# The first rows of a hybrid encoder layer: where g is copied, how squares are summed, and the order of the first products on TensorE

## The chip, the core and the metric

The kernel runs on one core of a Trainium2 chip. The metric is the device time of one execution in microseconds (us). Engines are named as the profile names them: PE (TensorE, matrix products), DVE (VectorE), ACT (ScalarE), POOL (GpSimd) and SP (SyncE, which issues most DMA transfers). Each takes its own instructions in order and waits on semaphores for the others.

## What is computed

One encoder layer on x of 512 rows by 1024 channels, in float32. Cut to the part that matters here:

```python
def rms_norm(x, g):
    y = x * rsqrt(mean(x * x, axis=-1, keepdims=True) + EPS)
    return y * g

n = rms_norm(x, mix_norm_g)
proj = n @ w_in                    # 512 x 1024 times 1024 x 4608
xa, zu, zv, gate_a, gate_b = split(proj)   # 512, 1024, 1024, 1024, 1024 columns
ya = s5_branch(xa, ...)            # two scans of a state-space model
yb = sgu_branch(zu, zv, ...)       # gelu, layer norm and mixing of positions
h = x + (sigmoid(gate_a) * (ya @ w_proj_a) + sigmoid(gate_b) * (yb @ w_proj_b)) @ w_out
# then memory cross-attention, a SwiGLU FFN and a last rms_norm
```

## The kernel before

**Products.** Every product is made of three matmuls: each operand is split into a high part (`hi`, a cast to fp32r by ACT) and a low part (`lo`, the rest, a subtraction by DVE), and `mm3` (L355) adds hi x hi, hi x lo and lo x hi in PSUM. `split` (L83) issues the two, one on each engine.

**Weights.** All weights come through one plan, a list of blocks of 512 KB in the order of use. A block is loaded by SP into `wraw` (three buffers), then split into `whi` and `wlo` (three buffers each). `next_w` (L330) hands out the next block, issues loads up to three blocks ahead and splits up to two ahead. The first four blocks of the plan are the first product's: rows 256 i to 256 i + 255 of `w_in`, columns of zv from 0 to 511. They are called blocks 0 to 3 below.

**Rows.** x is loaded in four row tiles of 128 rows, `xt[:, t, :]`, between the loads of the first three weight blocks (L566 to L571). Each row tile is normalised: ACT squares it and sums along the row (`sum_sq`, L483, two halves of 512, each with a read of the accumulator), DVE adds the two sums, scales and adds EPS, POOL takes the power -1/2 (`rms_factor`, L490), DVE multiplies by that factor and by g (`rms_scale`, L508). Then PE transposes its eight 128 x 128 pieces into two PSUM banks (`to_feat`, L514, tile `ptr`), and ACT and DVE split them into `xn`, the normalised rows with channels on partitions. The banks come from two rings: `bank` (five, for sums of products) and `aux` (three).

**g.** g arrives as one row (`g_row`). PE multiplies it by a column of ones (`pg`, L579), which spreads it over all partitions in two PSUM banks. ACT copies these to `g_mix` (L581 and L591) in between the steps of the first row tile. The first row tile is scaled straight from `pg` (L583), the three others from `g_mix` (L512).

**First products.** `tokm` (L399) computes zv's first 512 columns in four banks `pt`, one for each row tile: for each weight block it goes through the four row tiles, and through the last two blocks together. Gelu follows on ACT (`zv_evac`, L1019), then the products `pf` of `feat` (L362) for xa, and so on.

**Order.** A scheduler orders the instructions of each engine after the program is written, from its own model of the time; what `in_order` marks stays in the order of the program. While `pinned` is set, splits and squares are so marked: before, from the first row tile until the squares of the fourth. Transposes and first products were not marked, so the scheduler places them. In between it also places the set-up of the S5 branch (`s5_setup`, L620): small loads (`slab`, L631, the log steps; `lrows`; `brow`; `crow`), an exponential of `slab` on ACT (L672), small transposes on PE (`plam` L637, `pbc` L657 and L664) and many small operations on DVE.

Of the kernel before, what the change touches and what calls it, by code (L numbers as in the profile page):

```python
# [9 lines left out]
F32 = mybir.dt.float32  # L10
F32R = mybir.dt.float32r
AF = mybir.ActivationFunctionType
ALU = mybir.AluOpType
# [4 lines left out]
P = 128  # L18
D = 1024
T = 512  # L20
NT = T // P
KD = D // P
M = 256
NM = M // P
EPS = 1e-6
# [10 lines left out]
OFF_V = OFF_U + GW  # L36
# [16 lines left out]
def hybrid_layer_kernel(  # L53
# [17 lines left out]
    np_ = ctx.enter_context(tc.tile_pool(name="norm", bufs=2))  # L71
# [20 lines left out]
    pinned = [False]  # L92
    in_order = tc.keep_in_program_order
# [5 lines left out]
    plan, tiles = [], []  # L99
# [252 lines left out]
    def split_w(j):  # L352
        tiles.append(plan[j][2]())
# [45 lines left out]
    def tokm(w, c0, act, nk, evac, ntok=NT, last=2, kpt=2, hooks={}, cut=None, t0=0):  # L399


        toks = range(t0, t0 + ntok)
        ps = {t: bank(f"pt{t - t0}") for t in toks}
        nw = nk // kpt
        held = []
        full = slice(0, 512)
        for wi in range(nw):
            hi, lo = next_w(w, wi * kpt, kpt, c0, 512)
            held.append((wi, hi, lo))
            if wi in hooks:  # L410
                hooks[wi]()
            if wi < nw - last:
                todo, held = held, []
                for t in toks:
                    end = cut is not None and t == ntok - 1 and wi == nw - last - 1
                    tok_block(ps[t], t, todo, act, kpt, full, wi == 0, end)
                    if end:
                        cut(None, ps[t])
                tick(1.3 * ntok)
        for t in toks:  # L420
            if cut is not None and t == ntok - 1:
                for i in range(2):
                    p = aux("pcut", (P, 256))
                    tok_block(p, t, held, act, kpt, slice(256 * i, 256 * i + 256), True, True)
                    cut(i, p)
            else:
                tok_block(ps[t], t, held, act, kpt, full, nw == last, True)
                evac(t, ps[t])
            tick(1.3 * len(held))

    def tok_block(ps, t, ws, act, kpt, cs, first, final):
        tsl = slice(t * P, (t + 1) * P)
        for i, (wi, hi, lo) in enumerate(ws):
            for k in range(kpt):
                kk = wi * kpt + k
                mm3(ps, (act[0](kk, tsl), act[1](kk, tsl)) if callable(act[0]) else
                    (act[0][:, kk, tsl], act[1][:, kk, tsl]),
                    (hi[:, k, cs], lo[:, k, cs]), first and i == k == 0,
                    final and i == len(ws) - 1 and k == kpt - 1)

    side = {"gen": None, "credit": 0.0, "rate": 0.0, "now": 0, "later": []}

# [10 lines left out]
    def tick(us=5.2):  # L453

        side["now"] += us / 5.2
        run_due()
        side["credit"] = min(side["credit"] + us * side["rate"], us)
        while side["credit"] > 0.0 and side["gen"] is not None:
            try:
                used = next(side["gen"])  # L460
            except StopIteration:
                side["gen"] = None
                return
            if used is None:
                side["credit"] = 0.0
                return
            side["credit"] -= used
# [8 lines left out]
    ident = cp.tile([P, P], F32, name="ident")  # L476
# [13 lines left out]
    def rms_factor(ss, r=None):  # L490

        ms = np_.tile([P, 1], F32, tag="ms", name="ms", bufs=2)
        if r is None:
            r = np_.tile([P, 1], F32, tag="r", name="r", bufs=2)
        nc.vector.tensor_tensor(ms, ss[:, 0:1], ss[:, 1:2], ALU.add)
        nc.vector.tensor_scalar(ms, ms, 1.0 / D, EPS, ALU.mult, ALU.add)
        nc.gpsimd.tensor_tensor(r, ms, mhalf, ALU.pow)
        return r

    HALF = (slice(0, 512), slice(512, 1024))  # L500

    def row_sums(src):
        ss = np_.tile([P, 2], F32, tag="ss", name="ss", bufs=2)
        for i in range(2):
            sum_sq(ss[:, i:i + 1], src[:, HALF[i]])
        return ss

    def rms_scale(src, g, dst, ss=None):  # L508

        r = rms_factor(row_sums(src) if ss is None else ss)  # L510
        for i in range(2):
            nc.vector.scalar_tensor_tensor(dst[:, HALF[i]], src[:, HALF[i]], r, g[:, HALF[i]], ALU.mult, ALU.mult)  # L512

    def to_feat(src, hi, lo, tsl, full=None, skip=None, part=(0, 1)):  # L514

        for q in part:
            ps = aux("ptr", (P, 4, P))
            for j in range(4):
                k = 4 * q + j
                nc.tensor.transpose(ps[:, j, :], src[:, k * P:(k + 1) * P], ident)  # L520
            if q != skip:
                split(hi[:, 4 * q:4 * q + 4, tsl], lo[:, 4 * q:4 * q + 4, tsl], ps)
            if full is not None:
                nc.scalar.copy(full[:, 4 * q:4 * q + 4, tsl], ps)
# [13 lines left out]
    def slot(tag, shape, dt, name, place=NEAR):  # L538
        n = math.prod(shape[1:])
        t = sp.tile([P, KD * T + ROOM[tag]], dt, tag=tag, name=name)[:, place[tag]:place[tag] + n]  # L540
        return t.rearrange("p (a b c) -> p a b c", a=shape[1], b=shape[2]) if len(shape) == 4 else (
            t.rearrange("p (a b) -> p a b", a=shape[1]))
# [20 lines left out]
    g_mix = np_.tile([P, D], F32, tag="gain", name="g_mix", bufs=2)  # L563
    g_row = np_.tile([1, D], F32, tag="gain", name="g_row", bufs=2)
    nc.sync.dma_start(g_row, mix_norm_g)
    xt = slot("A", (P, NT, D), F32, "xt")  # L566
# [5 lines left out]
    xn_hi, xn_lo = token_slot("xn")  # L572
    xn = (xn_hi, xn_lo)

    def first_rows():

        pg = [aux("pg") for i in range(2)]
        for i in range(2):
            in_order(nc.tensor.matmul(pg[i], ones[0:1, :], g_row[:, HALF[i]], start=True, stop=True))  # L579
        r = rms_factor(row_sums(xt[:, 0, :]))  # L580
        in_order(nc.scalar.copy(g_mix[:, HALF[0]], pg[0]))  # L581
        for i in range(2):
            in_order(nc.vector.scalar_tensor_tensor(xt[:, 0, HALF[i]], xt[:, 0, HALF[i]], r, pg[i], ALU.mult, ALU.mult))  # L583
        raw = plan[0][3].pop("raw")
        hi = wp.tile([P, 2, 512], F32R, tag="hi", name="whi", bufs=3)
        lo = wp.tile([P, 2, 512], F32R, tag="lo", name="wlo", bufs=3)
        pinned[0] = True
        for q in range(2):
            split(hi[:, q, :], lo[:, q, :], raw[:, q, :])
            if q == 0:  # L590
                in_order(nc.scalar.copy(g_mix[:, HALF[1]], pg[1]))  # L591
            to_feat(xt[:, 0, :], xn_hi, xn_lo, slice(0, P), part=(q,))
        tiles.append((hi, lo))

    first_rows()
    split_w(1)
    ss = row_sums(xt[:, 1, :])
    for t in range(1, NT):
        rms_scale(xt[:, t, :], g_mix, xt[:, t, :], ss)
        if t == 1:  # L600
            ss = row_sums(xt[:, 2, :])
        to_feat(xt[:, t, :], xn_hi, xn_lo, slice(t * P, (t + 1) * P))
        if t == 1:
            ss3 = row_sums(xt[:, 3, :])
            pinned[0] = False
        if t == 2:
            ss = ss3

# [259 lines left out]
    turned = set()  # L868
# [150 lines left out]
    def zv_evac(half):  # L1019
        def f(t, ps):  # L1020
            nc.scalar.activation(zt[:, t, half * 512:(half + 1) * 512], ps, AF.Gelu_apprx_tanh,
                                 accum_out=zsum[:, t, half:half + 1])
        return f
# [2 lines left out]
    wsr, wst = wsx[:, 0], wsx[:, 1]  # L1026
    side["gen"] = s5_program()
    side["rate"] = RATE
    tokm(w_in, OFF_V, xn, KD, zv_evac(0))

    u = s5p.tile([P, G, NCH], F32, tag="u", name="u")

# [73 lines left out]
    for h in range(H):  # L1106
        ps = bank("psv")
# [73 lines left out]
    part = slot("A", (P, KD, T), F32, "part")  # L1181
# [216 lines left out]
    sums = []  # L1398
# [218 lines left out]
    ws = []  # L1617
# [241 lines left out]
```

## Time and profile before

| what | us |
|---|---|
| median of three runs | 878.69 |
| lowest and highest | 876.64, 880.33 |
| the profiled execution: device time | 877.4 |
| the profiled execution: its span | 875.6 |
| its stage of the first rows and first products, up to the first `pf` | 42.0 |

The span goes from the first to the last instruction that the profile shows; the device time has some 1.8 us around it. A row of the timeline gives start, length, engine, line, operation, output <- inputs, shape and count; equal neighbours are merged, and an "f32" shape of a matmul may be fp32r. Brackets give the idle time before an instruction and what ended it. A row of the chain gives start, length, and engine, tile and line. A row of waits gives who waited, for whom, the sum in us, how often, and the longest.

### The profile page before, as it was taken

What the parts mean: (1) busy time and instruction counts of PE and PEld (TensorE: products, weight loads), DVE (VectorE), ACT (ScalarE), POOL (GpSimd) and SP (SyncE); (2) the same over time, 40 slices, a digit from 0 to 9 for tenths busy, and PEclk for the clock granted to TensorE, in tenths of its full rate; (3) what the DMA queues carried; (4) which work ended last, traced back from release to release, by engine and by line L of the source; (5) the groups of instructions that cost most, each with busy time, mean ns of one, the idle gap of its engine ahead of it and who ended that gap; (6) DMA issues with size and microseconds to landing.
All of it is one profiled execution on the core that took longest, in us unless ns stands there. A gap on an engine that the chain in (4) does not pass through costs nothing.

```text
span 875.6 us, 14732 instructions
## 1 busy us (share of the span) xinstructions
PE 863.1 (99%) x5760; PEld 767.7 (88%) x5760; DVE 660.8 (75%) x1072; ACT 461.7 (53%) x688; POOL 88.6 (10%) x119
## 2 busy tenths in 40 slices
PE   9999999999999999999999999999999999999996
PEld 6788888888889988889899878999999999988875
DVE  5699885999846768568757746767877768899875
ACT  5643953244255643547546535545555555656664
POOL 1002201211020001100001001101111111000010
PEclk9999999999999999999999999999999999999998
DMA  8769565888663898724678545547999898366572
GB/s 253 200 187 292 112 171 149 192 230 198 161 194 110 267 314 246 252 93 161 207 239 240 157 128 158 148 144 172 218 235 235 208 234 217 97 191 207 193 238 98
DMA packets 116488, 169.56 MB, mean 194 GB/s; under 512 B 9265, under 2 KB 81473, under 8 KB 116290
## 3 DMA queue, kind: packets, MB, share of 16 engines
q1 hardware_dynamic: 96450, 140.59, 49.2%
q0 software_dynamic: 19680, 27.50, 19.8%
q8 instruction: 45, 0.74, 0.3%
q10 hardware_dynamic: 288, 0.52, 0.2%
q14 instruction: 25, 0.20, 0.1%
HBM read 159.71 MB, written 48.73 MB: 238 GB/s over the span
## 4 chain that ended last, share of the span: by engine, by line
PE 91%; DMA 4%; DVE 2%; ACT 1%; SPq 1%; issue 1%; POOLq 0%; ACTq 0%; DVEq 0%
PE pf L358 26%; PE pt L358 17%; PE px L1156 12%; PE dx L358 7%; PE pq L1156 6%; PE dq L358 3%; PE pv L1156 3%; PE dv L358 2%; PE pz L890 2%; PE qx L1156 2%; PE bx L1156 1%; DMA e<-ed 1%; PE ptr L520 1%; PE po L358 1%; DMA slab<-in_s_log_step_dram 1%; DMA wraw<-qsum 1%
## 5 line engine op out<-in xcount | busy, mean ns | idle before, releaser
L85 ACT CAST whi<-wraw 128x1024 fp32r<-128x1024 f32 (+1 forms) x145 | 148.5, 1025 | 158.5 <-PE pf L358 54.7
L86 DVE TENSOR_TENSOR wlo<-wraw,whi 128x1024 fp32r<-128x1024 f32 (+1 forms) x145 | 172.0, 1189 | 67.1 <-ACT whi L85 66.4
L358 PE MATMUL pf<-xn,whi 128*128 128x512 f32 x448 | 140.2, 392 | 0.0
L358 PEld LDWEIGHTS pf<-xn,whi 128*128 128x128 f32 x448 | 83.7, 188 | 17.3 <-issue 0.4
L358 PE MATMUL pf<-xn,wlo 128*128 128x512 f32 x224 | 87.6, 392 | 0.0
L1156 PE MATMUL px<-fn,whi 128*128 128x256 f32 x480 | 83.3, 276 | 0.0
L1156 PEld LDWEIGHTS px<-fn,whi 128*128 128x128 f32 x480 | 72.5, 188 | 0.2
L86 DVE TENSOR_TENSOR wlo<-b,whi 128x1024 fp32r<-128x1024 f32 x40 | 48.9, 1223 | 27.8 <-ACT whi L85 27.8
L85 ACT CAST whi<-b 128x1024 fp32r<-128x1024 f32 x40 | 42.2, 1054 | 50.8 <-PE px L1156 27.7
L1156 PE MATMUL px<-fn,wlo 128*128 128x256 f32 x240 | 66.4, 277 | 0.0
L1156 PE MATMUL pq<-s,whi 128*128 128x256 f32 x320 | 55.0, 276 | 0.0
L358 PE MATMUL dx<-whi,s 128*128 128x512 f32 x170 | 53.4, 391 | 0.4 <-DVE h L1784 0.4
L86 DVE TENSOR_TENSOR wlo<-t,whi 128x1024 fp32r<-128x1024 f32 x30 | 36.7, 1225 | 19.4 <-ACT whi L85 19.4
L85 ACT CAST whi<-t 128x1024 fp32r<-128x1024 f32 x30 | 31.6, 1054 | 35.3 <-PE pv L1156 12.4
L358 PEld LDWEIGHTS pf<-xn,wlo 128*128 128x128 f32 x224 | 42.1, 188 | 8.8 <-issue 0.2
L1156 PEld LDWEIGHTS pq<-s,whi 128*128 128x128 f32 x320 | 48.1, 188 | 0.0
L358 PE MATMUL pt<-whi,xn 128*128 128x512 f32 x128 | 44.5, 415 | 0.8 <-ACT xn L85 0.8
L1156 PEld LDWEIGHTS px<-fn,wlo 128*128 128x128 f32 x240 | 45.1, 188 | 0.0
L1156 PE MATMUL pq<-s,wlo 128*128 128x256 f32 x160 | 44.2, 276 | 0.0
L358 PEld LDWEIGHTS dx<-whi,s 128*128 128x128 f32 x170 | 31.8, 188 | 7.6 <-issue 0.8
L358 PE MATMUL dx<-wlo,s 128*128 128x512 f32 x85 | 32.9, 389 | 0.0
L358 PEld LDWEIGHTS pt<-whi,xn 128*128 128x128 f32 x128 | 24.6, 195 | 6.8 <-ACT xn L85 1.4
(453 smaller groups left out, 2197.5 us busy)
## 6 DMA issues: line engine op xcount, KB each, us to landing
wraw<-in_w_in_dram SPq DMA_DIRECT2D x36, 512.0 KB, 4.9
dsum<-in_w_down_dram SPq DMA_DIRECT2D x20, 512.0 KB, 5.8
wraw<-dsum SPq DMA_DIRECT2D x20, 512.0 KB, 3.6
b<-in_w_gate_dram SPq DMA_DIRECT2D x15, 512.0 KB, 5.6
b<-in_w_up_dram SPq DMA_DIRECT2D x15, 512.0 KB, 4.6
wraw<-in_w_down_dram SPq DMA_DIRECT2D x15, 512.0 KB, 4.3
dsum<-in_w_down_dram POOLq DMA_DIRECT2D x10, 512.0 KB, 7.1
dsum<-dsum POOLq DMA_DIRECT2D x10, 512.0 KB, 8.1
```

The lines of the kernel that those rows point to most:

```text
L85: hi = nc.scalar.copy(dst_hi, src)
L86: lo = nc.vector.tensor_tensor(dst_lo, src, dst_hi.bitcast(F32), ALU.subtract)
L358: m = nc.tensor.matmul(ps, a[x], b[y], start=start and i == 0, stop=stop and i == 2, skip_group_check=free)
L520: nc.tensor.transpose(ps[:, j, :], src[:, k * P:(k + 1) * P], ident)
L890: nc.tensor.matmul(ps[:, g, :], wt[:, g, :], u[:, o * GO + g, :], start=True, stop=True)
L1156: nc.tensor.matmul(ps[:, j, :], a[x], b[y], start=start and j == k == i == 0, stop=k == 3 and i == 2, skip_group_check=True)
```

## The change

Five things change, all in the first 42 us.

- The two copies of g to `g_mix` leave the first row tile. They come behind the second row tile's splits and block 2's split (new L624). The second row tile is scaled from `pg`, as the first.
- Row tiles 2, 3 and 4 are squared in one operation of 1024 elements each (`whole_sum`), with one accumulator read, and the addition of two sums on DVE falls away. The squares themselves go to `sums`, which takes a large slot of SBUF (E) that the tile `wsx` uses afterwards.
- The first products and the transposes of row tiles 2 to 4 are marked to stay in the order of the program on PE, and that order goes by row tiles: blocks 0 and 1 with tile 1; transposes of tile 2; blocks 0 and 1 with tile 2; block 2 with tiles 1 and 2; transposes of tile 3; blocks 0 to 2 with tile 3; transposes of tile 4; blocks 0 to 2 with tile 4, and then block 3 with all four (these last two left to the scheduler).
- Block 2 is split after the second row tile's split instead of ahead of it.
- For the first two row tiles the second half's transposes take a bank of `bank`, since `pg` keeps two of `aux`.

```diff
-    def tok_block(ps, t, ws, act, kpt, cs, first, final):
+    def tok_block(ps, t, ws, act, kpt, cs, first, final, turn=False):
...
-                    final and i == len(ws) - 1 and k == kpt - 1)
+                    final and i == len(ws) - 1 and k == kpt - 1, turn=turn)
...
-        nc.vector.tensor_tensor(ms, ss[:, 0:1], ss[:, 1:2], ALU.add)
-        nc.vector.tensor_scalar(ms, ms, 1.0 / D, EPS, ALU.mult, ALU.add)
+        if ss.shape[1] > 1:
+            nc.vector.tensor_tensor(ms, ss[:, 0:1], ss[:, 1:2], ALU.add)
+        nc.vector.tensor_scalar(ms, ms if ss.shape[1] > 1 else ss, 1.0 / D, EPS, ALU.mult, ALU.add)
...
+    pg = [aux("pg") for i in range(2)]
+
     def first_rows():
-        pg = [aux("pg") for i in range(2)]
...
-        in_order(nc.scalar.copy(g_mix[:, HALF[0]], pg[0]))
...
-            if q == 0:
-                in_order(nc.scalar.copy(g_mix[:, HALF[1]], pg[1]))
-            to_feat(xt[:, 0, :], xn_hi, xn_lo, slice(0, P), part=(q,))
+            to_feat(xt[:, 0, :], xn_hi, xn_lo, slice(0, P), part=(q,), rings=(aux, bank))
...
     first_rows()
+    sums = slot("E", (P, NT, D), F32, "sums")
+
+    def whole_sum(t):
+        ss = np_.tile([P, 1], F32, tag="ss", name="ss", bufs=2)
+        in_order(nc.scalar.activation(sums[:, t, :], xt[:, t, :], AF.Square, accum_out=ss))
+        return ss
+
+    pt = {t: bank(f"pt{t}") for t in range(NT)}
+
+    def first_product(t, wi):
+        tok_block(pt[t], t, [(wi,) + tiles[wi]], xn, 2, slice(0, 512), wi == 0, False, True)
+
+    def first_feat(t, rings=None):
+        to_feat(xt[:, t, :], xn_hi, xn_lo, slice(t * P, (t + 1) * P), rings=rings, turned=True)
+
     split_w(1)
-    ss = row_sums(xt[:, 1, :])
-    for t in range(1, NT):
-        rms_scale(xt[:, t, :], g_mix, xt[:, t, :], ss)
-        if t == 1:
-            ss = row_sums(xt[:, 2, :])
-        to_feat(xt[:, t, :], xn_hi, xn_lo, slice(t * P, (t + 1) * P))
-        if t == 1:
-            ss3 = row_sums(xt[:, 3, :])
-            pinned[0] = False
-        if t == 2:
-            ss = ss3
+    ss1 = whole_sum(1)
+    rms_scale(xt[:, 1, :], pg, xt[:, 1, :], ss1)
+    ss2 = whole_sum(2)
+    for wi in range(2):
+        first_product(0, wi)
+    first_feat(1, (aux, bank))
+    split_w(2)
+    for i in range(2):
+        in_order(nc.scalar.copy(g_mix[:, HALF[i]], pg[i]))
+    rms_scale(xt[:, 2, :], g_mix, xt[:, 2, :], ss2)
+    for wi in range(2):
+        first_product(1, wi)
+    ss3 = whole_sum(3)
+    for t in range(2):
+        first_product(t, 2)
+    first_feat(2)
+    pinned[0] = False
+    rms_scale(xt[:, 3, :], g_mix, xt[:, 3, :], ss3)
+    for wi in range(3):
+        first_product(2, wi)
+    first_feat(3)
...
-    tokm(w_in, OFF_V, xn, KD, zv_evac(0))
+    for wi in range(3):
+        w = next_w(w_in, wi * 2, 2, OFF_V, 512)
+        tok_block(pt[3], 3, [(wi,) + w], xn, 2, slice(0, 512), wi == 0, False)
+        tick(6.9)
+    w = next_w(w_in, 6, 2, OFF_V, 512)
+    evac = zv_evac(0)
+    for t in range(NT):
+        tok_block(pt[t], t, [(3,) + w], xn, 2, slice(0, 512), False, True)
+        evac(t, pt[t])
+        tick(1.3)
```

`rms_scale` takes a list of two tiles as g as well, and marks its scalings while `pinned` is set; `to_feat` takes the rings (`rings`) of its two banks and marks its transposes when `turned`.

More of the change, by code (lines that the diff above doesn't have):

```diff
@@ L511, in rms_scale, with to_feat @@
         for i in range(2):
-            nc.vector.scalar_tensor_tensor(dst[:, HALF[i]], src[:, HALF[i]], r, g[:, HALF[i]], ALU.mult, ALU.mult)
-    def to_feat(src, hi, lo, tsl, full=None, skip=None, part=(0, 1)):
+            scaled = nc.vector.scalar_tensor_tensor(dst[:, HALF[i]], src[:, HALF[i]], r,
+                                                    g[i] if isinstance(g, list) else g[:, HALF[i]], ALU.mult, ALU.mult)
+            if pinned[0]:
+                in_order(scaled)
+    def to_feat(src, hi, lo, tsl, full=None, skip=None, part=(0, 1), rings=None, turned=False):
+        rings = rings or (aux, aux)
         for q in part:
-            ps = aux("ptr", (P, 4, P))
+            ps = rings[q]("ptr").rearrange("p (j c) -> p j c", j=4)
             for j in range(4):
                 k = 4 * q + j
-                nc.tensor.transpose(ps[:, j, :], src[:, k * P:(k + 1) * P], ident)
+                m = nc.tensor.transpose(ps[:, j, :], src[:, k * P:(k + 1) * P], ident)
+                if turned:
+                    in_order(m)
             if q != skip:
```

## The prediction

> **What bounds the kernel now.** I read the page first: its span and its row of busy times.
>
> ```profile
> span 875.6 us, 14732 instructions
> PE 863.1 (99%) x5760; PEld 767.7 (88%) x5760; DVE 660.8 (75%) x1072; ACT 461.7 (53%) x688; POOL 88.6 (10%) x119
> ```
>
> TensorE (PE) is busy 863.1 of 875.6 us, so at most 12.5 us are left for any reordering that keeps its work. Second, the list of what PE waited for, over the whole span.
>
> ```profile
> PE idle L556 <- DVE mhalf L481: 1.1, 1, 1.1
> PE py L946 <- DMA tt<-kd: 1.0, 1, 1.0
> PE pt L358 <- ACT ot_hi L85: 0.9, 2, 0.7
> PE pt L358 <- ACT xn L85: 0.8, 1, 0.8
> ```
>
> The only wait in the stage of this change is the last row: 0.8 us before a first product (`pt`) whose rows (`xn`) ACT had not yet cast. Third, the chain that ended last, followed through the first stage, with the time after it.
>
> ```profile
> 6.07 9.91 DMA slab<-in_s_log_step_dram
> ...
> 16.07 0.11 ACT slab L672
> ...
> 16.21 0.58 ACT xn L85
> ...
> 16.83 5.52 PE pt L358 x23
> 22.35 1.31 PE ptr L520 x12
> ...
> 31.11 1.02 PE pbc L657 x8
> ...
> 36.70 5.47 PE pt L358 x24
> 42.17 17.91 PE pf L358 x79
> ```
>
> This decides the case. What sets 16.83 us is neither the copies of g nor the squares, but a small load of S5 parameters (`slab`): issued at 6.07, 9.91 us under way. ACT's exponential of it stands ahead of the casts of the second row tile in ACT's order, so those casts start at 16.21. From 16.83 on PE runs to the end with the short waits above. The change is therefore worth what it does to (a) the work PE has behind it at 16.83 and (b) PE's gaps between 16.83 and 42. A product's matmul costs 5.47 / 24 = 0.228 us of PE there, a transpose 1.31 / 12 = 0.109.
>
> Last, the timeline of the second row tile, all engines.
>
> ```profile
> 11.42 0.65 ACT L486 ACTIVATE sq<-xt 128x512 f32<-128x512 f32 x1
> ...
> 12.57 0.20 ACT L486 ACTIVATION_READ_ACCUMULATOR sq<-xt 128x1 f32 x1
> 12.80 0.16 DVE L495 TENSOR_TENSOR ms<-ss 128x1 f32<-128x1 f32 x1
> ...
> 12.92 1.04 ACT L85 CAST whi<-wraw 128x1024 fp32r<-128x1024 f32 x1
> 13.00 0.15 DVE L496 TENSOR_SCALAR ms<-ms 128x1 f32<-128x1 f32 x1
> ...
> 13.82 1.42 DVE L512 SCALAR_TENSOR_TENSOR xt<-xt,r,g_mix 128x512 f32<-128x512 f32 x2 [0.67 <-POOL r L497]
> ...
> 15.15 1.22 DVE L86 TENSOR_TENSOR wlo<-wraw,whi 128x1024 fp32r<-128x1024 f32 x1
> ...
> 16.07 0.23 ACT L672 ACTIVATE slab<-slab 128x32 f32<-128x32 f32 x1 [0.86 <-DMA slab<-in_s_log_step_dram]
> 16.80 0.69 DVE L86 TENSOR_TENSOR xn<-ptr,xn 128x512 fp32r<-128x512 f32 x1 [0.36 <-ACT xn L85]
> ```
>
> Squares of a row tile take ACT from 11.42 to 12.77, and before the load lands ACT sits idle for 0.86 us.
>
> **The change part by part.** In the built program of the changed kernel I read the order of each engine; no time is in it.
>
> *First row tile.* The two copies of g leave ACT's head. Their rows:
>
> ```profile
> 6.03 0.58 ACT L581 COPY g_mix<-pg 128x512 f32<-128x512 f32 x1 [0.75 <-PE pg L579]
> 6.72 0.75 DVE L583 SCALAR_TENSOR_TENSOR xt<-xt,r,pg 128x512 f32<-128x512 f32 x1 [1.06 <-ACT g_mix L581]
> 7.74 0.75 DVE L583 SCALAR_TENSOR_TENSOR xt<-xt,r,pg 128x512 f32<-128x512 f32 x1 [0.27 <-PE pg L579]
> 8.52 0.58 ACT L591 COPY g_mix<-pg 128x512 f32<-128x512 f32 x1 [0.34 <-DVE xt L583]
> ```
>
> The first copy held the first scaling to 6.72, but the second scaling is released by PE's product `pg` at 7.74 whatever ACT does. The second copy pushed the first cast of `xn` to about 9.0; without it that cast can start some 0.3 us earlier. Gain: at most 0.3 us on the first product, and it ends in the wait for `slab`: counted 0.
>
> *Squares in one operation.* Two reads of the accumulator become one (0.20) and DVE's addition goes (0.16); the wider square itself should cost about two narrow ones. The scaling reads `pg` in PSUM instead of g_mix, 0.75 against 0.71 a half. The second tile is scaled some 0.2 us sooner, at about 15.0. Its casts still stand behind the exponential of `slab` on ACT, and the eight loads ahead of `slab` on SP's queue are unchanged, so it lands at 16.0 again. Counted 0; cover gone, this would be worth up to 0.3 us.
>
> *PE's order up to 16.83.* Rows of PE before, from this point and from the third tile:
>
> ```profile
> 9.65 0.79 PE L358 MATMUL pt<-whi,xn 128*128 128x512 f32 x1
> ...
> 11.95 1.05 PE L358 MATMUL pt<-whi,xn 128*128 128x512 f32 x2
> 12.86 0.80 PE L358 MATMUL pt<-wlo,xn 128*128 128x512 f32 x1
> 13.45 0.87 PE L358 MATMUL pt<-whi,xn 128*128 128x512 f32 x2
> ...
> 14.40 0.62 PE L358 MATMUL pt<-whi,xn 128*128 128x512 f32 x2
> 14.86 1.16 PE L520 MATMUL ptr<-ident,xt 128*128 128x128 f32 x8
> ...
> 17.16 0.63 PE L358 MATMUL pt<-wlo,xn 128*128 128x512 f32 x2
> ...
> 22.18 1.47 PE L520 MATMUL ptr<-ident,xt 128*128 128x128 f32 x12
> 22.82 1.56 ACT L85 CAST xn<-ptr 128x512 fp32r<-128x512 f32 x3 [4.33 <-PE ptr L520]
> 23.44 1.89 DVE L86 TENSOR_TENSOR xn<-ptr,xn 128x512 fp32r<-128x512 f32 x3 [1.22 <-ACT xn L85]
> 23.46 0.50 PE L358 MATMUL pt<-whi,xn 128*128 128x512 f32 x1
> ```
>
> Before, PE had issued 13 products and 8 transposes by 14.86 + 1.16; the scheduler had put one product of weight block 2 ahead of the transposes. Now the order is fixed: 12 products (blocks 0 and 1), 8 transposes. One matmul is still owed at 16.83: +0.23.
>
> *Weight block 2.* Its cast (12.92, 1.04) and its low part on DVE (15.15, 1.22) lay in the shadow of the `slab` wait. Now they come after the second tile's casts: ACT 17.3 to 18.3, DVE 18.4 to 19.6. Their reader is the product after twelve matmuls from 16.83, at 16.83 + 12 x 0.228 = 19.6 plus the gap below: just hidden. If it is not, each tenth of lateness is a tenth of the span. But before, products of block 2 filled PE while DVE made the second tile's low part. Now the third product needs that low part, ready at 16.80 + 0.69 = 17.49 against 16.83 + 0.46 = 17.29: a gap of about 0.25.
>
> *Tiles three and four.* Each one's transposes now stand directly ahead of its own products. From the rows: first transpose to end of the first cast is 22.18 to about 23.4, to the first product 23.46: 1.28 us; eight transposes fill 8 x 0.109 = 0.87 (12 in 1.31 before). So 0.41 us gap. The low part follows 0.70 us after, two products cover 0.45: 0.25 more. Together 0.66 a tile. Before, the third tile hid this behind twelve transposes and kept perhaps 0.15; the fourth hid it wholly. Now: +0.5 for the third; +0.45 for the fourth, where a small transpose of S5 (`plam`) fills part. Bounds of each: 0 (if PE's modelled ends hide slack) and 0.9 (if ACT is late by another square).
>
> *Fewer changes of kind.* Eight `pbc` took 1.02 for 0.87 of streaming: 0.15 for one interruption; the new order has one fewer: -0.15.
>
> *g copies, squares of tile four, loads.* On ACT the copies (2 x 0.58) and the square (about 1.3) follow block 2's cast, 18.3 to 20.8; DVE scales tile three at 19.6 to 21.0 and PE asks for it at about 22.5: hidden by 1.5 us. The load of `wsx` now waits for that last square because it takes its place in SBUF, some 3 us later; its reader on PE (`pws`) starts at 135.9.
>
> ```profile
> L1073 PE MATMUL pws<-ident,wsx x8: 270/272/273, 135.9 to 139.9; 128*128 128x128 f32 x8
> ```
>
> Behind it on SP's queue stand the load of `mix` and the next weight blocks, which wait for DVE to free their places anyway (block 2's low part and later ones); POOL's queue only gets its power for tile three earlier, ahead of the same transfers. Hidden. **Sum:** 0.23 + 0.25 + 0.5 + 0.45 - 0.15 = +1.3 us at 42 us, rounded down to +1.2 because the first tile starts a little earlier. The profiled execution took 877.4 us, 1.8 around its span; it becomes 878.6. The median of the three runs, 878.69, lies 1.3 above the profiled one, so the forecast on it is **879.9 us**, 0.14% more.
>
> *The clock.* Products up to 13.45 start 0.427 us apart (two in 1.05), from 14.40 on 0.23 (two in 0.62): PE ran at half rate until about 14. Before this costs nothing, since the `slab` wait swallows it. After, PE has an estimated stall of 0.4 us near 12.2 (its seventh matmul starts 0.3 us sooner, and the low part of block 1 comes only after its cast and 1.2 us on DVE) in the stretch in which the rate doubled.
> The Trainium skill, "TensorE: Matmul & The Clock Gate", section "Part 1: The HAM clock gate", says that the clock doubles only after a free-running window of about 3.4 us of sustained work. The row agrees (no gap over 0.2 us between 9.65 and 13.9); taken strictly, a stall in that window would put the doubling into the next unbroken one, which begins at 16.83; by that rule the sum would be the first rival's.
>
> **The rivals.**
> 1. *The clock stays low past 16.83.* Place: the second tile's products. Price: 0.2 us per matmul (0.427 against 0.228). Eight such matmuls (3.4 us) give +1.6: 881.5 us, chance 0.15. The same mechanism decides the sign beyond the bound of 0.5% (4.4 us) when sixteen or more run at half rate, through the gaps of tile three up to about 24: 1.2 + 24 x 0.2 = +6, minus the gaps it hides: 884 us, **slower**, chance 0.07. For: all three gaps fall into this stretch. Against: before, the 0.8 us of idle PE ahead of 16.83 did not lower it.
> 2. *The order pays.* PE's gaps at tiles three and four overlap better than my serial reading (casts and transposes of two halves in two banks) and the earlier first tile survives: -0.5 us, 878.2, chance 0.15. Over 0.5% it cannot bring: all that PE loses between 9.65 and 16.83, idle or at half rate, is 7.18 - 13 x 0.228 - 8 x 0.109 = 3.3 us, and the `slab` wait keeps most of it.
> 3. *Nothing arrives at the end.* A shift of 1.2 us is swallowed by the DMA waits later (`tt<-kd` 1.0): 878.7, chance 0.13. Against: that load is itself issued after PE work.
>
> **How the numbers follow.** Forecast 0.5; rivals 0.15 and 0.07, 0.15, 0.13. A difference under 0.5% is about what a measurement of this kernel can tell from no change; the three runs before span 876.64 to 880.33. Range 877.2 to 882.7: the lower end is rival 2 less 1.0 of scatter, the upper end rival 1's milder form plus 1.2. Slower by over 0.5%: 0.08 (rival 1's strong form and a point for an unseen stall); faster by over 0.5%: 0.04 (an order effect later on that I do not see); within: 0.88.
>
> **What would show it.** In the changed profile: the exponential of `slab` again ends ACT's wait near 16.0, and the casts of `xn` follow it; the first product of tile two at 16.8; gaps of some 0.4 and 0.25 us ahead of the first and third product of tiles three and four; first `pf` at 43 to 43.5. Wrong if: the casts start before 15.5, products after 16.83 are 0.4 us apart, or PE shows a wait of over 1 us after 45.

## The result, and the profile after

The changed kernel took 884.80 us in the median of nine runs (880.48 to 889.01), the kernel before 878.35 us (nine runs, 875.54 to 880.33): ratio 1.0078, 95% interval 1.0061 to 1.0095. Two later measurements gave 1.0068 (1.0044 to 1.0091) and 1.0051 (1.0032 to 1.0071). So by the medians the change costs 3.9 to 6.5 us where the forecast was +1.2, and the time lies outside the range of 877.2 to 882.7. The profiled execution, 880.48 us with a span of 878.7, is the fastest of its nine: read it for places, not for the whole loss.

The row of busy times after:

```profile
span 878.7 us, 14723 instructions
PE 863.8 (98%) x5760; PEld 767.8 (87%) x5760; DVE 659.8 (75%) x1069; ACT 461.0 (52%) x682; POOL 86.8 (10%) x119
```

PE still bounds the kernel. Its longest waits (engine, tile, line, for whom: us in all, times, longest):

```profile
PE ptr L525 <- DVE xt L590: 1.6, 1, 1.6
...
PE pt L358 <- ACT xn L85: 1.1, 2, 0.8
PE pt L358 <- ACT ot_hi L85: 0.9, 2, 0.7
...
PE pt L358 <- DVE ms L497: 0.5, 1, 0.5
```

The first of them ends at 7.61 us, where the transposes began at 7.63 before, so it costs nothing. Behind 45 us no single wait is over 0.8 us.

The chain through the first stage (start, length, what):

```profile
6.43 8.93 DMA slab<-in_s_log_step_dram
...
15.44 0.23 ACT slab L702
15.67 0.48 ACT xn L85
...
16.19 6.04 PE pt L358 x24
22.23 0.45 PE ptr L525 x4
...
23.34 4.64 PE pt L358 x18
...
37.22 5.48 PE pt L358 x24
```

The first stage is as the prediction drew it: the load of `slab` gates the casts, then come 24 products where 23 were (6.04 us for 5.52) and a gap before tile three. From the exponential of `slab` to the first `pf` it is 42.54 - 15.44 = 27.10 us; before, 42.01 - 16.07 = 25.94. That is +1.16, against +1.2 to 1.3 in the sum. Term by term, by the steps from one start to the next: one matmul 0.23, and gaps that grew by 0.27 at tile two, 0.43 at tile three and 0.16 at tile four (predicted 0.25, 0.5 and 0.45).

The rest is elsewhere. Groups of products between 269 and 548 us, before and then after (count | busy us, mean ns of one | idle):

```profile
L358 PE MATMUL pt<-whi,mg_lo 128*128 128x512 f32 x64 | 24.8, 391 | 0.0
L358 PE MATMUL pt<-whi,mg_hi 128*128 128x512 f32 x64 | 24.3, 389 | 0.0
...
L1156 PE MATMUL bx<-yb_lo,whi 128*128 128x256 f32 x48 | 13.3, 278 | 0.0
...
L1156 PE MATMUL qq<-hse,whi 128*128 128x256 f32 x48 | 10.1, 276 | 0.0
```

```profile
L358 PE MATMUL pt<-whi,mg_lo 128*128 128x512 f32 x64 | 25.2, 396 | 0.0
L358 PE MATMUL pt<-whi,mg_hi 128*128 128x512 f32 x64 | 24.6, 395 | 0.0
...
L1195 PE MATMUL bx<-yb_lo,whi 128*128 128x256 f32 x48 | 13.5, 282 | 0.0
...
L1195 PE MATMUL qq<-hse,whi 128*128 128x256 f32 x48 | 10.3, 282 | 0.0
```

Same instructions, same order, no wait: each matmul takes 4 to 6 ns longer, and the median distance from one start to the next grows from 227 to 233 ns (512 wide) and from 113 to 120 (256 wide). Only products that read a tile of slot D or E do this: `yb`, `hsd` and `hse` (sums of the normalised h), `mg`, `ot`. In the built programs the two slots have changed places. Slots are laid out in the order in which they are first used; before, D came first (with `zt`), at byte 104000, and E (with `wsx`) after it; with `sums` in E, E comes first and D moves to 120448. The offsets inside the slots (L535, L536 before) stayed, so the start addresses modulo 256 bytes moved: `yb`, `hsd`, `hse` (the moving operand) from 0 to 64, `mg` and `ot` (the stationary one) from 64 to 128. Their partners, the weights `whi` and `wlo`, stay at 64.

In the table, "exchanged" means that E is placed ahead of D, and "kept" that D is first, as before. It gives the same matmuls' starts, less those of the profiled execution before, in us, for one profiled execution of each kernel:

| kernel | exponential of slab | first pf | at 60 | at 175 | at 340 | at 600 |
|---|---|---|---|---|---|---|
| before | 16.07 | 42.01 | 0 | 0 | 0 | 0 |
| changed | 15.44 | 42.54 | +0.5 | +0.5 | +0.6 | +2.5 |
| changed (e9) | 14.91 | 41.96 | -0.1 | 0.0 | +0.5 | +2.4 |
| exchanged, sums in D (e11) | 17.13 | 45.59 | +3.6 | +3.6 | +4.1 | +6.1 |
| before, slots exchanged (e2) | 16.40 | 42.33 | +0.3 | +0.3 | +1.3 | +3.1 |
| kept, sums in E (e12) | 15.48 | 42.60 | +0.6 | +0.6 | +0.9 | +1.2 |
| kept, sums in D (e10) | 15.03 | 42.15 | +0.1 | +0.4 | +1.8 | +0.9 |

Exchanged kernels lose 1.8 to 2.0 us between 340 and 600; kept ones lose 0.3 or win 0.9. One profile of before is a thin base: ten of the thirteen profiles in which all these operands have their old start addresses modulo 256 bytes (before, e1, e5 to e8, e10, e12, e13, e15 to e18) win 0.8 to 1.0 us in that stretch. From 175 to 600, which takes in the products of `yb`, the thirteen move by -0.6 us on average (-1.6 to +1.0), and the five exchanged ones (changed, e2, e4, e9, e11) by +2.5 (+2.0 to +3.0): 3.1 us apart.

### The profile page after: what moved, and what is told of

The parts are those of the page before. It is cut to its first block, busy times and chain, and to the rows that moved or that the text cites. A ratio compares the mean times of both kernels' runs of the same rounds, so it can differ in the third digit from the quotient of the medians.

```text
span 878.7 us, 14723 instructions
## 1 busy us (share of the span) xinstructions
PE 863.8 (98%) x5760; PEld 767.8 (87%) x5760; DVE 659.8 (75%) x1069; ACT 461.0 (52%) x682; POOL 86.8 (10%) x119
## 4 chain that ended last, share of the span: by engine, by line
PE 89%; DMA 5%; DVE 3%; ACT 2%; issue 1%; SPq 1%; POOLq 0%; ACTq 0%; DVEq 0%
PE pf L358 26%; PE pt L358 18%; PE px L1195 12%; PE pq L1195 6%; PE dx L358 5%; PE dq L358 3%; PE pv L1195 3%; PE dv L358 2%; PE pz L920 2%; PE qx L1195 2%; PE bx L1195 1%; DMA e<-ed 1%; DVE wlo L86 1%; PE po L358 1%; PE ptr L525 1%; DMA wraw<-dsum 1%
```

## Experiments

Theory after the result: the exchange of D and E makes the large part, the new order of the first rows the predicted 1.2, and the late load of `slab` with a falling clock the rest. Rivals: the order alone; the load of `wsx` held by the squares; the places themselves and not the remainders. Ratios are to the kernel before, measured beside each, with 95% intervals.

**e1, the sums in D.** D is then first, as before; nothing else changes.

```diff
-    sums = slot("E", (P, NT, D), F32, "sums")
+    sums = slot("D", (P, NT, D), F32, "sums")
```

> The changed kernel with one word altered: the tile of squares, sums, takes slot D instead of slot E, so that D is the first of the two to get a place in SBUF, as in the kernel before. Theory of the place: the change let E take its place ahead of D, so the two slots changed places (D from byte 104000 to 120448, E from 120576 to 104000), and products that read tiles there are issued wider apart. Then this kernel is back at the kernel before plus the 0.5 to 1.2 us of the first stage: ratio 1.001 (0.999 to 1.003), about 879.3 us, with products of mg issued every 0.227 us. Rival, the order: what the fixed order moved (side work, loads) costs the time; then this kernel is as slow as the changed one: ratio 1.0078, about 884.8 us, first pf at 42.5 in both.

Measured: 1.0019 (0.9997 to 1.0042), median 880.46 us against 877.59; products back at 227 and 113 ns, first `pf` at 41.80 with `slab` used at 14.27. The changed kernel, measured beside it (e4), had 1.0068: most of the loss goes with the places.

**e2, the exchange alone.** The kernel before, in which E is touched first.

```diff
+    nc.gpsimd.memset(slot("E", (P, 1, 16), F32, "first"), 0.0)
     def first_rows():
```

> The kernel before with one small addition: 16 columns of slot E are set to zero by POOL ahead of the first rows, so that slot E takes its place ahead of slot D; order and work of the first rows are those of before. Theory of the place: ratio 1.005 to 1.008, about 883.5 us, products of mg every 0.233 us, first pf still at 42.0. Rival, the order: ratio 1.000 (0.998 to 1.002), about 878.4 us, products of mg every 0.227 us.

Measured: 1.0039 (1.0023 to 1.0055), 880.92 us. Two of its groups:

```profile
L358 PE MATMUL pt<-whi,mg_lo 128*128 128x512 f32 x64 | 25.2, 396 | 0.0
...
L1158 PE MATMUL qq<-hse,whi 128*128 128x256 f32 x48 | 10.4, 282 | 0.0
```

A memset of 16 columns, with the old first rows, costs 3.4 us: the exchange is a cause by itself. It is less than the 1.005 to 1.008 expected, so it isn't the whole loss. The memset is not what costs: e12 has one of the same size, in D, and no such loss.

**e3, remainders restored in part.** The changed kernel with the offsets of D and E exchanged as well.

```diff
-    ROOM = {"A": 0, "B": 48, "C": 16, "D": 48, "E": 16}
-    NEAR, AWAY = {..., "D": 0, "E": 16}, {..., "D": 48, "E": 0}
+    ROOM = {"A": 0, "B": 48, "C": 16, "D": 16, "E": 48}
+    NEAR, AWAY = {..., "D": 16, "E": 0}, {..., "D": 0, "E": 48}
```

> The changed kernel with slots D and E still exchanged, but with the spare columns of the two and the offsets of tiles in them exchanged too, so that each tile starts at the same remainder of 256 bytes as in the kernel before, 16 KB from where it was. Theory of the place, if the remainder decides: ratio 1.001, about 879.3 us, as when sums takes slot D. If the place itself (which 16 KB) decides: ratio 1.0078, about 884.8 us. Rival, the order: 1.0078 as well.

Measured: 1.0044 (1.0020 to 1.0069). `mg`, `ot` and `yb` are back; the sums of h are not:

```profile
L358 PE MATMUL pt<-whi,mg_lo 128*128 128x512 f32 x64 | 24.8, 391 | 0.0
...
L1195 PE MATMUL qq<-hse,whi 128*128 128x256 f32 x48 | 10.3, 281 | 0.0
```

`hsd` and `hse` have offsets of their own (L1385 to L1388 of the kernel before), which this edit left: they start at 192 and 64. The rule holds tile by tile, but the kernel isn't restored; e13 does it.

**e4, the changed kernel again.**

> The changed kernel unaltered, for a second profile: the first one was of its fastest run (880.48 us), 4.3 us below its median. Ratio 1.0078 again. Theory of the place: a slower run shows still wider steps, or more of them, in the products that read slots D and E (mg, ot, yb, and the sums beside it), and no new wait. Rival, the order: the added 4 us stand as waits of PE between 42 and 300 us.

Measured: 1.0068 (1.0044 to 1.0091). Its profiled execution took 890.33 us and shows something new. Chain, and four stretches of the clock's own length (us; busy us and count of PE, PEld, DVE, ACT, POOL; granted clock; DMA share; GB/s):

```profile
6.40 10.87 DMA slab<-in_s_log_step_dram
...
17.35 0.23 ACT slab L702
17.58 0.48 ACT xn L85
...
18.10 8.61 PE pt L358 x24
```

```profile
10.58:13.99 3.41, 2.65 (x11) 1.54 (x9) 2.53 (x5) 2.98 (x5) 0.55 (x1) 1.00 1.08 322
14.00:17.41 3.41, 1.49 (x9) 0.84 (x8) 0.93 (x3) 0.06 (x1) 0.55 (x1) 1.00 0.88 127
17.41:20.82 3.41, 2.72 (x6) 2.11 (x7) 2.59 (x4) 3.41 (x7) 0.00 (x0) 0.50 0.81 165
20.82:24.23 3.41, 3.41 (x9) 2.64 (x8) 2.68 (x5) 0.69 (x2) 0.55 (x1) 0.50 1.05 299
```

The load landed 1.9 us later than in the first profile. In the stretch before 17.41 PE was busy 1.49 of 3.41 us, and then the clock was granted at half for 6.8 us: 24 products in 8.61 us for 6.04. The first `pf` came at 47.02. Later, at 105.7, PE waited 2.5 us for ACT (behind POOL and a late transfer), and the clock fell once more, for 3.4 us.

**e5 to e8, what is left with kept places.** All four are e1, except e6, which is the kernel before. e5 and e6 move the load of `slab` to ACT's queue:

```diff
     nc.scalar.dma_start(xt[:, 0, HALF[1]], x[0:P, HALF[1]])
+    slab = s5p.tile([P, 32, G], F32, tag="wt", name="slab", bufs=2)
+    for d in range(2):
+        nc.scalar.dma_start(slab[64 * d:64 * d + 64, 0, :], s5_log_step[0, d].partition_broadcast(64))
...
-        slab = s5p.tile([P, 32, G], F32, tag="wt", name="slab", bufs=2)
...
-        for d in range(2):
-            nc.sync.dma_start(ls[64 * d:64 * d + 64, :], s5_log_step[0, d].partition_broadcast(64))
```

> The changed kernel with sums in slot D, and in it the load of the S5 log steps (slab) issued on ACT's queue right behind the first row tile's half, instead of behind eight loads on SP's queue. Theory (the late load holds ACT's exponential, the casts of row tile two and PE, and in some executions the idle PE then falls back to half rate): ACT no longer waits for it, the casts of tile two start at about 14.5, the first pf starts 0.5 to 1 us sooner than the 41.80 of the kernel with sums in D alone, and the median falls from 880.5 to about 878.5, with hardly a run above 882. Rival (the fixed order itself or something later makes the runs above 880): the first pf moves as said, the median stays within 1 us of 880.5.

Measured: 1.0012 (0.9998 to 1.0026), median 878.72, no run above 880.5. The load is off the path, as ACT's first cast of tile two shows, which now waits for the transposes:

```profile
15.65 1.23 ACT L85 CAST xn<-ptr 128x512 fp32r<-128x512 f32 x2 [1.41 <-PE ptr L525]
```

The first `pf` did not come sooner, though (42.64): the transposes themselves were 0.8 us later than in e1, and ACT's first cast of weight block 0 had to wait for its load until 8.48 us (e1: 6.63). In e6 and e18, which have the early load too, that cast started at 9.12 and 8.96, before at 7.57. So the early load doesn't leave the rest as it was. The spread is smaller here: standard deviation 1.1 us where e1 has 2.4.

> The kernel before with the same early load of slab alone. Theory (PE before had other work, weight block 2's products, so little was lost to the load): first pf 0.2 to 0.5 us sooner than 42.0, median 877 to 877.5. Rival (the wait for slab costs the kernel before as much as the changed one): 1 us or more sooner, median 876.5 or less. Both say that the products of w_out stay at 227 ns, as no tile moves in SBUF.

Measured: 1.0001 (0.9988 to 1.0014), 877.93 us; standard deviation 0.9 where the kernel before has 1.5. Both theories expected a sooner first `pf` and a gain in the median; neither came. In the profile the first `pf` was later, at 43.80: PE waited 1.2 us for the first cast of `xn`, which ACT could start only at 10.24 (9.00 before), ran at half rate until 16.59 (13.97 before) and waited 0.4 us for the cast of weight block 2. Measured side by side, e5 and e6 both have the early load; they differ by 0.0011, 1.0 us, for the new first rows with kept places. Both intervals include 1.

e7 leaves PE's order to the scheduler again:

```diff
-        tok_block(pt[t], t, [(wi,) + tiles[wi]], xn, 2, slice(0, 512), wi == 0, False, True)
+        tok_block(pt[t], t, [(wi,) + tiles[wi]], xn, 2, slice(0, 512), wi == 0, False)
...
-        to_feat(xt[:, t, :], xn_hi, xn_lo, slice(t * P, (t + 1) * P), rings=rings, turned=True)
+        to_feat(xt[:, t, :], xn_hi, xn_lo, slice(t * P, (t + 1) * P), rings=rings)
```

> The changed kernel with sums in slot D, and PE's order of the first products and transposes left to the scheduler again; the squares, the sums and the order of ACT and DVE stay changed. Theory of the prediction (the fixed order costs gaps ahead of tiles three and four): first pf 0.5 to 0.9 us sooner than 41.80 for the same landing of slab, median 879.5 to 880. Rival (the order costs nothing; what is left of the loss is elsewhere): first pf within 0.2 us, median 880.5.

Measured: 1.0011 (0.9994 to 1.0029), 879.12 us. In its profile `slab` landed late (17.32), the clock fell to half from 18.56 to 21.97, and PE was 3.0 us behind the kernel before at 60 us (the first `pf` can't be compared, since the scheduler put it at 40.02, among the first products): 1.25 of later landing, about 2.0 of half rate (24 products in 7.49 us for 5.5), and so nothing for the order. With the fixed order and the same event, e11 was 3.6 behind: 1.06 of landing, 1.3 of half rate (7.38 us for 6.04), 1.2 left. In the median the two orders can't be told apart.

e8 puts four spare products into the wait:

```diff
+    def first_product_spare():
+        hi, lo = tiles[0]
+        for k in range(2):
+            m = nc.tensor.matmul(pt[3], xn_hi[:, k, 0:P], hi[:, k, :], start=True, stop=True)
+            in_order(m)
...
     first_feat(1, (aux, bank))
+    for i in range(2):
+        first_product_spare()
```

> The changed kernel with sums in slot D, and four spare products (into the bank of row tile four, which is written anew later, so the output is the same) between the transposes and the first product of row tile two, where PE waits for the late load. They take 0.9 us of a wait of 1 to 2.5 us. Theory (idle PE in that wait drops the clock in some executions, and this makes the runs above 882): the profile shows the first pf within 0.3 us of 41.80, the median falls to 879 or less, and the spread of the runs narrows to that of the kernel before. Rival (the clock in the first stage makes no part of the spread): median within 1 us of 880.5, same spread.

Measured: 1.0011 (0.9993 to 1.0030), 878.45 us, but two of twelve runs above 882 and a standard deviation of 1.9. It is not decisive: the median fell as the theory said, the spread hardly.

**e9 to e12, a square.** D and E exchanged or kept, the sums in E or in D. In e11 a memset of 16 columns of E stands ahead of the sums in D, in e12 one of D ahead of the sums in E.

> The changed kernel again, as the first corner of a square of four kernels on one chip (D and E exchanged or not, the sums in slot E or in slot D): exchanged, sums in E. All theories: ratio to the kernel before about 1.007, as in the two measurements so far.

> Second corner: places kept, sums in slot D (the changed kernel with sums in D, measured once at 1.0019). Theory (the exchanged places are the large loss, the new order a small one): about 1.0015, products of w_out 227 ns apart.

> Third corner: a memset of 16 columns of slot E ahead of the sums places E first, as in the changed kernel, but the sums are in slot D, so that the load of wsx waits for nothing of the first rows. Theory (the exchanged places alone): as the changed kernel, 1.006 to 1.007, products of w_out 233 ns apart. Rival (the load of wsx, held by the last square, delays SP's queue and what follows it): as the second corner, 1.0015.

> Fourth corner: a memset of 16 columns of slot D ahead of the sums keeps the places as they were, and the sums are in slot E as the change has them. Theory (the exchanged places alone): as the second corner, 1.0015, products of w_out 227 ns apart. Rival (the held load of wsx): 1.005 to 1.007 with products 227 ns apart.

| | sums in E | sums in D |
|---|---|---|
| exchanged | e9: 1.0051 (1.0032 to 1.0071) | e11: 1.0067 (1.0042 to 1.0091) |
| kept | e12: 1.0022 (1.0000 to 1.0045) | e10: 1.0028 (1.0002 to 1.0053) |

The rows differ by 0.0034, 3.0 us; the columns by nothing that shows. So the held load of `wsx` falls. One group each of e11 and e12:

```profile
L358 PE MATMUL pt<-whi,mg_lo 128*128 128x512 f32 x64 | 25.2, 396 | 0.0
```

```profile
L358 PE MATMUL pt<-whi,mg_lo 128*128 128x512 f32 x64 | 24.8, 391 | 0.0
```

**e13, all remainders restored, places exchanged.** e3, and the offsets of the sums of h exchanged too:

```diff
-    hops[6], hops[5] = halves_at(sd, 4, 256, APART), halves_at(se, 4, 256, (0, 64))
-    hops[3] = (part_at(sd, 2176 + APART[0]), part_at(se, 2048 + 64))
+    hops[6], hops[5] = halves_at(sd, 4, 256, (0, 64)), halves_at(se, 4, 256, APART)
+    hops[3] = (part_at(sd, 2176), part_at(se, 2176 + APART[0]))
```

> The changed kernel with D and E exchanged as it has them, but the offsets inside both slots set so that every tile in them that TensorE reads (yb, the split sums of hn, mg, ot) starts at the same remainder modulo 256 bytes as in the kernel before. Theory (the remainders, not the places, widen the products): w_out and w_xo at 227 ns, yb and the sums of hn at 113 ns, and the ratio to the kernel before at that of the two kernels with kept places, 1.0025. Rival (the place itself, or the neighbours in SBUF): products stay at 233 and 120 ns where they are exchanged, ratio 1.005 to 1.007.

Measured: 1.0027 (1.0008 to 1.0046), as the kept kernels, and

```profile
L358 PE MATMUL pt<-whi,mg_lo 128*128 128x512 f32 x64 | 24.8, 391 | 0.0
...
L1195 PE MATMUL qq<-hse,whi 128*128 128x256 f32 x48 | 10.0, 276 | 0.0
```

**e14, remainders moved, places kept, first rows of before.**

```diff
-    NEAR, AWAY = {..., "D": 0, "E": 16}, {..., "D": 48, "E": 0}
+    NEAR, AWAY = {..., "D": 16, "E": 16}, {..., "D": 0, "E": 16}
```

> The kernel before, nothing exchanged and its first rows untouched, with three offsets changed: in D the near one from 0 to 16 columns (mg_lo and ot_hi then start at remainder 128 instead of 64) and the far one from 48 to 0, in E the far one from 0 to 16 (both halves of yb at 64 instead of 0). mg_hi, ot_lo and the sums of hn stay. Theory of the remainders: within one product of w_out the matmuls of mg_lo take 233 ns and those of mg_hi 227; of w_xo those of ot_hi 233, those of ot_lo 227; yb 120, the sums of hn 113. In time 64 x 6 ns + 128 x 6 ns = 1.2 us, and up to 1.3 for yb (192 x 7 ns): ratio 1.001 to 1.003, with the first pf where it was. Rival: no spacing changes.

Measured: 1.0015 (1.0000 to 1.0029). Within one product, the tile that moved is slow and its partner is not:

```profile
L358 PE MATMUL pt<-whi,mg_lo 128*128 128x512 f32 x64 | 25.3, 398 | 0.0
...
L358 PE MATMUL pt<-whi,mg_hi 128*128 128x512 f32 x64 | 24.3, 390 | 0.0
...
L1156 PE MATMUL bx<-yb_lo,whi 128*128 128x256 f32 x48 | 13.5, 282 | 0.0
...
L1156 PE MATMUL qq<-hse,whi 128*128 128x256 f32 x48 | 10.0, 276 | 0.0
```

Start to start the picture is less sharp than expected: 236 ns after `mg_lo`, 228 and 229 after `mg_hi`, and 232 after `ot_lo`, which I had put at 227. Together e13 and e14 settle it for the pace: the remainder (the start address modulo 256 bytes) decides, not the place. Its profile also shows, with the old first rows, a load that landed at 17.7 and the clock at half from 18.31 on:

```profile
14.90:18.31 3.41, 1.37 (x9) 1.07 (x9) 2.00 (x3) 2.86 (x7) 0.00 (x0) 1.00 0.30 70
18.31:21.72 3.41, 3.23 (x8) 2.59 (x9) 2.89 (x7) 1.84 (x6) 0.55 (x1) 0.50 0.80 174
```

So the falling clock isn't the change's own: the kernel before has it too when the load is late enough.

**e15 to e18, the load of slab behind the other S5 loads.** e15 is the kernel before, e16 is e12; in both the two loads move behind those of `crow`.

> The kernel before with the load of slab behind the loads of the other S5 parameters, so that its exponential stands behind the casts of row tile two in ACT's order. Theory (the load gates PE at row tile two in the kernel before too): casts of tile two start at about 15.7, as soon as the transposes allow, first pf 0.4 to 0.6 us sooner than 42.0, median 877 to 877.5. Rival (something else is ready no sooner): first pf within 0.2 us.

Measured: 0.9985 (0.9971 to 0.9999), 876.85 us against 878.01, no run above 878.4, first `pf` at 41.17. ACT now casts tile two first and waits for the load where nobody waits for ACT:

```profile
15.32 1.31 ACT L85 CAST xn<-ptr 128x512 fp32r<-128x512 f32 x2 [0.29 <-PE ptr L520]
...
19.96 0.23 ACT L672 ACTIVATE slab<-slab 128x32 f32<-128x32 f32 x1 [2.09 <-DMA slab<-in_s_log_step_dram]
```

> The changed kernel with kept places and the sums in E (measured at 1.0022), with the same later load of slab. Theory (what is left of the loss is the wait for slab, with the fall to half rate in executions where it lands late): casts of tile two at 14.5 to 14.8 in every execution, no half rate after 12 us, first pf at 41.5 to 41.9, and the ratio at 1.000 or below. Rival (the gaps of the fixed order make the rest): ratio stays at 1.002.

Measured: 1.0026 (1.0003 to 1.0049). It doesn't decide: the load landed at 22.7, and the exponential stood ahead of the casts of tile three, so the wait had only moved, and the standard deviation was the largest of all, 3.3 us. The granted clock of every run goes with it: the five runs at 0.997 or more took 876.3 to 877.9 us, the seven at 0.996 or less 879.3 to 885.5. The moved wait:

```profile
23.45 0.50 PE L358 MATMUL pt<-whi,xn 128*128 128x512 f32 x1 [1.43 <-ACT xn L85]
```

> The kernel before with the load of slab behind the other S5 loads, again, as the only version so far below the kernel before. If its 0.9985 was no accident of that chip, 0.997 to 1.000 again with all runs below 879.5, since PE no longer waits for the load and never falls to half rate; if it was, 1.000 to 1.001 with the spread of the kernel before.

Measured: 0.9993 (0.9981 to 1.0005), 876.58 us against 877.21, all runs below 878.2. Both medians are below the kernel before, but only e15's interval leaves out 1.

> The changed kernel with kept places (sums in slot D) and the early load of slab, again: 1.0012 before, with no run above 882. Theory (with places kept and the load off the path, only the new order of the first rows is left, some 0.7 to 1.2 us): 1.0005 to 1.0015, no run above 882. Rival (the new first rows themselves make the spread): 1.002 or more, with runs above 882.

Measured: 1.0013 (0.9998 to 1.0029), 878.55 us, one run of twelve at 883.79. With places kept and the load off the path 1.1 us are left, the size of the predicted order, but the interval includes 1 and reaches 2.5 us. The standard deviation is 1.9, so the narrow spread of e5, the same kernel, did not come again. In e18's profile full rate began at 14.07 and in e5's at 11.80, and the first `pf` came at 43.13 and 42.64.

## Why the prediction was wrong

**The step that failed** is "Hidden", for the squares' place in SBUF. The working asked who waits for `wsx`, found its reader on PE only at 135.9, and that part is right (the columns of the square don't differ). It did not ask what else a new first user of slot E does: it reorders the slots, and with them the start addresses of four operands (`yb`, the sums of h, `mg`, `ot`) read from 269 to 548 us. By durations that is 384 matmuls of 512 columns x 5 ns + 336 of 256 x 6 ns = 3.9 us, of which some at `yb` vanish in waits for loads; measured, 3.4 us alone (e2), 3.0 in the square, 3.1 between the profiles. The order of the instructions cannot show it, since there no instruction moves; the addresses can. None of the prediction's signs of being wrong could have caught it either: it makes no wait, only wider steps.

**The fixed order: right in size by the profile, not shown in the median.** One matmul and the gaps came to +1.16 us by the profile, for +1.2 in the sum. Two errors in the terms cancel there, which is luck: tile four lost 0.16 for 0.45, and the saving of 0.15 from fewer changes of kind did not show. In the medians, e5 against e6 gives 1.0 us and e18 1.1, but all their intervals include 1, and e7, without the fixed order, has the same 1.0011.

**First row tile and squares: right at nothing.** The casts of tile two waited for the load all the same (2.1 us of idle ACT before 15.44), so an earlier scaling bought nothing.

**"So it lands at 16.0 again": wrong as a fixed number.** In the fourteen profiles with the load at its old place, ACT could use `slab` at 14.3 to 17.7. With the new first rows, use at 14.3 (e1) puts the first `pf` 0.2 us ahead of before, and use at 17.1 (e11) 3.6 behind.

**The rival of the low clock: right as a mechanism, wrong in its trigger.** I had it start with a stall near 12.2. The stall came (0.54 us ahead of 12.58), but full rate had begun at 11.10 and stayed. What stood ahead of the falls at tile two is the wait for `slab`. The "against" in the prediction, that 0.8 us of idle PE had not lowered the clock, held only for a load at 16. The fall came in e4, e7, e11 and e14, and costs 1.3 to 2.6 us at tile two. These are the four of the fourteen profiles in which `slab` was used at 17.1 or later; the other ten, at 16.4 or earlier, don't have it. That the new first rows lose more clock than the kernel before is shown by the granted clocks of all runs: 0.9970 on average in 161 runs of the kernel before, 0.9962 in 104 of the nine measurements with the new first rows, the fixed order and the load at its old place (standard errors 0.0001 and 0.0002). The difference is worth an estimated 0.75 us (0.00085 of 880). Where in the run they lose it is not shown, and e8 and e18 have runs above 882 in spite of their cover. The rival's strong form named 884 us, and the median was 884.80: that is luck, since the exchange makes 3.0 to 3.4 of it.

The Trainium skill, "TensorE: Matmul & The Clock Gate", section "Part 1: The HAM clock gate", puts the fall to half rate after an idle window of about 3.4 us. The rows of e4 and e14 agree in the length (half rate comes in pieces of 3.41 us), but PE was busy 1.49 and 1.37 us in the stretch before. The Trainium skill, on the same page, section "Part 4: PE-mode transpose", says that transposes don't count as a busy PE in the same way; that would fit, since the eight transposes of tile two make 1.27 of the 1.49. But the later fall in e4, at 106.15, came after 0.95 us of work with no such transpose in it, so no run here separates the two.

**Sum.** Exchange 3.0 to 3.4 us, order 1.1 to 1.2, and in kept kernels (1.0019 to 1.0028) another 0.5 to 1.3, which is what is left over: 4.6 to 5.9, against 3.9 to 6.5 measured. Of the three, the exchange is shown by runs; the order is read from one pair of profiles; the rest is put down to late loads and the clock, whose mean supports 0.75 of it. Left open are the spread that remains in e18 and the cause of the wait at 105.7 in e4, which was read but not tried. A further source of spread was not tried: in the twenty profiles, the last start of full rate ahead of the second row tile's products lies anywhere from 10.6 to 16.6 us.

## What to carry to other kernels

Before pricing a change by its order, compare the addresses of every tile that the bounding engine reads, before and after: a scratch tile in a shared slot can shift operands hundreds of microseconds away. A small load whose consumer stands in an in-order queue ahead of critical casts makes the time depend on when it lands: put its consumer behind them (e15: 0.9985, e17: 0.9993, the only version here below the kernel before; small, and within the interval in e17). And look at several executions before taking a landing time as a constant.

## What the hardware showed that was not expected

- The start address of an operand in SBUF, modulo 256 bytes, changes the pace of fp32r matmuls: 512 columns with the moving operand at 64 take 227 ns with the stationary one at 64 and 233 with it at 128; 256 columns with the stationary operand at 64 take 113 ns with the moving one at 0 and 120 with it at 64 (119 at 192, in e3). No run changed another pair, and why the address matters is not shown.
- A granted clock at full rate was lost at tile two after stretches of 3.41 us in which PE was busy 0.8 to 1.5 us (e4, e7, e11, e14), and kept after one with 2.59, 14.51 to 17.92, in the changed kernel's first profile:

```profile
14.51:17.92 3.41, 2.59 (x13) 1.58 (x11) 1.82 (x5) 2.48 (x5) 0.55 (x1) 1.00 1.02 160
```

Busy time alone doesn't decide it: in the same profile full rate was granted from 4.27 and lost at 7.69, after a stretch with 1.86 us, and e16 kept it after one with 2.00 (21.08 to 24.50) and lost it after one with 2.05 (4.02 to 7.43).
